# Input-row loads and mixer-row stores of 114 rows issued as 112 rows and 2 rows

## The chip, the core and the metric

The kernel runs on one core of one Trainium2 chip, as one program in one launch. The metric is the device time in microseconds; the time of before is the median of 3 runs. Five engines work side by side, each on its own instructions in order: PE (TensorE, matrix products into PSUM, with its weight loads PEld), DVE (VectorE), ACT (ScalarE), POOL (GpSimd) and SP (SyncE, which here only issues transfers between DRAM and the on-chip buffers). Engines wait for one another and for transfers by semaphores.

## What is computed

One layer of a hybrid decoder on 1024 rows of 1024 columns, with 16 learned rows ahead of them, all in float32. A mixer (a gated recurrence and a multi-window pooling, merged by sigmoid gates) gives `z`; its product with `w_out` is normalised and added to the input rows, and a gated FFN with a causal convolution of width 3 follows:

```python
h = jnp.concatenate([meta, x], axis=1)
...
z = (jax.nn.sigmoid(gate_a.astype(jnp.float32)) * (a @ w_branch_hgrn[l])
     + jax.nn.sigmoid(gate_b.astype(jnp.float32)) * (p @ w_branch_pool[l]))
h = h + rmsnorm(z @ w_out[l], mix_norm_post[l])
u = rmsnorm(h, ffn_norm_pre[l])
gt = causal_dwconv(u @ ffn_w_gate[l], ffn_conv_w[l], ffn_conv_b[l])
y = (jax.nn.gelu(gt, approximate=True) * (u @ ffn_w_up[l])) @ ffn_w_down[l]
h = h + rmsnorm(y, ffn_norm_post[l])
return h[:, N_META:]
```

## The kernel before

Every float32 product is made of three products of a split: an operand is cast to a high part (`hi`) by ACT, and DVE or POOL subtracts it from the operand for the low part (`lo`); `mm3` then issues hi-hi, hi-lo and lo-hi (L160 to L162, or L262 to L265 in the Strassen products).

The kernel goes through four stages: the projections and the recurrence (to about 600 us), the mixer's product with `w_out` (600 to about 730 us), the FFN's gate and up products in Strassen form (to about 1190 us), and the down product with the last norm.

The stage that matters is the second. Only 1026 of the 1040 rows are wanted from here on (`TQ`: the 1024 output rows and 2 rows of halo for the convolution). They are cut into three thirds of 342 rows (`c`), and each third into three row tiles of 342 / 3 = 114 rows (`RT`).

- `load_res` (L1000) loads the 114 input rows of a row tile, `row2` (written `row` in the profile), three tiles at the start of each third, called from `mix_mm`. The first tile of all takes 2 rows of `meta_tokens` and 112 of `x`.
- `mix_mm` (L1055) runs the third's product: for each of the 8 blocks `k` of `z` it takes a 128x1024 block of `w_out` (`wsplit`, L131: load `wraw`, cast `whi` on ACT, subtract `wlo` on POOL, on DVE for the last two), and 18 matmuls of 128x512 over the three row tiles into PSUM pairs `pm`. The blocks come from a `Loader` that is 3 ahead; `wraw`, `whi` and `wlo` have 3 buffers each. The blocks of `z` are split too (`split_z`, L935: `zc`), into the buffers of one large pool of 24 ("fm") that nearly everything shares, `m1`, `un` and `row2` too.
- `mix_out` (L1077) empties a third's PSUM pairs: ACT squares and sums a row tile (L1085, `junk`), DVE multiplies by the gain into `m1` (L1086, `m`). Two closures for each row tile follow, which are worked off between the blocks `k` of the next third: `vec` (L1090) forms the norm, adds the input rows (L1095), stores the 114 rows to the DRAM scratch `hs` (L1096, `hscr`) and normalises again to `un` (L340, L345); `feat` (L1099, by `to_quarters`) transposes `un` on PE (L1017, `pt`) and splits the result into the operands of the FFN (`v`, `t1` to `t4`, by `put`, L324 to L327, and L1032 to L1053).
- The last third's closures run between the first products of the FFN (`ffn.start_pair`), whose results DVE adds (`put_ffn`, L1191).
- The scratch `hs` is read back at the very end (`load_h`, L1351), 128 rows at a time.

All loads and stores named here are issued by SP, in one queue. The order of the rows on each engine is chosen by a scheduler that plays the program on a model of the chip; by hand it is fixed only in the first stage, and for POOL in the FFN. A change of any instruction can therefore move others.

Of the kernel before, what the change touches and what calls it, by code (L numbers as in the profile page):

```python
# [20 lines left out]
HALO = 2  # L21
# [35 lines left out]
def trunk_kernel(ctx: ExitStack, tc: tile.TileContext, x, meta_tokens, mix_norm_pre,  # L57
# [3 lines left out]
    nc = tc.nc  # L61
# [26 lines left out]
    def slot(n, dtype=F32, name="s"):  # L88
        return stage["fm", "p"].tile([P, n], dtype, tag="fm", name=nm(name), padded_shape=[P, L])
# [10 lines left out]
    def pair_banks(name="pt"):  # L100
        t = pair(name)
        return t[:, :512], t[:, 512:]
# [4 lines left out]
    def small(shape, name, tag, bufs=4):  # L107
        return sm.tile(shape, F32, tag=tag, name=nm(name), bufs=bufs)
# [55 lines left out]
    def proj(w, col, n_k, xs, chunks, ws=None, name="pj"):  # L164

        if ws is None:
            ws = wsplit(wblock(w, 0, n_k, col, P), n_k, P)
        whi, wlo = ws
        banks = [bank(name) for _ in chunks]
        for k in range(n_k):  # L170
            for (lo, n), ps in zip(chunks, banks):
                xhi, xlo = xs(k, lo, n)
                pe.matmul(ps[:, :n], whi[:, k, :], xhi, start=(k == 0), stop=False)
                pe.matmul(ps[:, :n], whi[:, k, :], xlo, start=False, stop=False)  # L174
            for (lo, n), ps in zip(chunks, banks):
                xhi, _ = xs(k, lo, n)
                pe.matmul(ps[:, :n], wlo[:, k, :], xhi, start=False, stop=(k == n_k - 1))
        return banks
# [151 lines left out]
    def row_rstd(ssq, rows, tag):  # L330
        std = small([P, 1], "std", tag + "s")
        act.activation(std[:rows], ssq[:rows], AF.Sqrt, bias=eps_t[:rows], scale=1.0 / D)
        rstd = small([P, 1], "rstd", tag + "r")
        dve.reciprocal(rstd[:rows], std[:rows])
        return rstd
# [12 lines left out]
    def norm_rows(row, rows, gbc):  # L348
        return list(norm_steps(row, rows, gbc))[-1]
# [498 lines left out]
    with tc.manual_schedule(engines={E.Activation, E.DVE, E.PE}):  # L848
# [59 lines left out]
        for h in range(EARLY_G):  # L908
            src, n_k, xs, chunks, post = job("G", h)
            r = proj(None, 0, n_k, xs, chunks, ws=gl.next(), name="pg")  # L910
# [65 lines left out]
    hs = dram.tile([TQ, D], F32, name="hscr")  # L976
# [11 lines left out]
    def add_quarters(*names):  # L988
        for q in names:
            for h in "hl":  # L990
# [4 lines left out]
    RT = CW // 3  # L995

    wo = Loader([(wblock(w_out[0], k, 1, 0, D), 1, D, dve if (c == 2 and k > 5) else pool_e)
                 for c in range(3) for k in range(KD)])

    def load_res(t0):  # L1000
        row = slot(D, name="row2")
        if t0 == 0:
            nc.sync.dma_start(row[:HALO], meta_tokens[T0:NM, :])
            nc.sync.dma_start(row[HALO:RT], x[0, 0 : RT - HALO, :])
        else:
            nc.sync.dma_start(row[:RT], x[0, t0 - HALO : t0 - HALO + RT, :])
        return row

    def t_tmp(n, name):
        return slot(n, name=nm(name))  # L1010

    def to_quarters(un, t_at, banks):

        for j in range(2):
            for i in range(4):
                k = 4 * j + i
                pe.transpose(banks[j][:, i * RT : (i + 1) * RT], un[:RT, k * P : (k + 1) * P], ident[:RT, :RT])  # L1017
        srcs = [b_[:, : 4 * RT].rearrange("p (k t) -> p k t", k=4) for b_ in banks]
        n1 = max(0, min(RT, HT - t_at))
        if n1:  # L1020
            for src, q in zip(srcs, ("b11", "b21")):
                put(q, src[:, :, :n1], slice(t_at, t_at + n1), dve)
        f = max(0, HT - HALO - t_at)
        n2 = RT - f
        if n2 <= 0:
            return
        d = slice(t_at + f - (HT - HALO), t_at + RT - (HT - HALO))
        b12, b22 = (src[:, :, f:] for src in srcs)

        t1, t2 = halves_tmp(n2)  # L1030
        c12, c22 = halves_tmp(n2)
        act.copy(c12, b12)  # L1032
        act.copy(c22, b22)
        combine(dve, t1, c12, ALU.subtract, "b11", d)
        dve.tensor_tensor(t2, c22, t1, ALU.subtract)
        put("t2", t2, d, dve)
        dve.tensor_tensor(c12, c22, c12, ALU.subtract)
        put("t1", t1, d, dve)
        put("b22", c22, d, pool_e)
        put("t3", c12, d, dve)  # L1040
        negdiff(t2, t2, "b21", d)
        return lambda: put("t4", t2, d, pool_e)
# [12 lines left out]
    def mix_mm(c, between, zs):  # L1055
        rows.update({c * CW + i * RT: load_res(c * CW + i * RT) for i in range(3)})
        banks = [pair_banks("pm") for _ in range(3)]
        znext = []
        for k in range(KD):
            whi, wlo = wo.next()  # L1060
            if k == KD - 1 and c < 2:
                znext = [split_z(c + 1, k_) for k_ in range(ZA)]
            zh, zl = zs[k]
            for i in range(3):
                t = slice(i * RT, (i + 1) * RT)
                for j in range(2):
                    n = slice(j * 512, (j + 1) * 512)
                    mm3(banks[i][j][:RT], (zh[:, t], zl[:, t]), (whi[:, 0, n], wlo[:, 0, n]), k == 0, k == KD - 1)
            wo.ahead()
            if k + ZA < KD:  # L1070
                zs.append(split_z(c, k + ZA))
            if between:
                for f in between.pop(0):
                    f()
        return banks, znext

    def mix_out(c, banks, g2, g3):  # L1077
        todo = []
        for i in range(3):
            m1 = slot(D, name="m1")  # L1080
            ssq = small([P, 2], "ssq2", "mq", 6)
            for j in range(2):
                n = slice(j * 512, (j + 1) * 512)
                junk = t_tmp(512, "junk")
                act.activation(junk[:RT], banks[i][j][:RT], AF.Square, accum_out=ssq[:RT, j : j + 1])  # L1085
                dve.tensor_tensor(m1[:RT, n], banks[i][j][:RT], g2[:RT, n], ALU.mult)  # L1086
            un = {}
            t0 = c * CW + i * RT

            def vec(i=i, m1=m1, ssq=ssq, un=un, t0=t0):  # L1090
                row = rows.pop(t0)
                s = small([P, 1], "mss", "ms")
                dve.tensor_tensor(s[:RT], ssq[:RT, 0:1], ssq[:RT, 1:2], ALU.add)
                rstd = row_rstd(s, RT, "m")
                dve.scalar_tensor_tensor(m1[:RT], m1[:RT], rstd[:RT], row[:RT], ALU.mult, ALU.add)  # L1095
                nc.sync.dma_start(hs[t0 : t0 + RT, :], m1[:RT])  # L1096
                un[0] = norm_rows(m1, RT, g3)

            def feat(un=un, t0=t0):  # L1099
                return to_quarters(un[0], t0, pair_banks())  # L1100

            todo += [vec, feat]
        return todo
# [325 lines left out]
```

## Time and profile before

| | |
|---|---|
| median of 3 runs | 1434.69 us (1431.66 to 1434.87) |
| profiled execution | 1431.93 us, its span 1430.1 us |
| mean granted PE clock | 0.979 |
| stores `hscr<-m` | 9 of 456 KB |
| loads `row<-in_x_dram` of `load_res` | 8 of 456 KB, 1 of 448 KB |
| 512 KB blocks of `w_out` | 24, landing after 3.1 to 20.3 us |

A profile line of the timeline gives the start (us from the span's start), the length in us, the engine, the line of the code, the operation, what is written and read (buffer numbers left out), and the count of merged instructions; in brackets the idle time of the engine before it and what ended that. SPq is SP's queue of issues: its lengths are those of the issue, not of the transfer.

### The profile page before, as it was taken

How to read it: one execution, taken by the hardware profiler on the slowest of the kernel's cores; microseconds unless marked ns; L12 is line 12 of the kernel's file. 1: busy time of each engine (PE TensorE's matmuls, PEld its weight loads, DVE VectorE, ACT ScalarE, POOL GpSimd, SP SyncE). 2: the span in 40 equal slices, each digit the busy share in tenths (PEclk: the TensorE clock that was granted, in tenths of full speed). 3: DMA queues.
4: the chain of work that ended last, by engine and by line, in shares of the span. 5: the costliest groups of instructions: out<-in, count | busy, mean ns of one | idle time of the engine just before them, and what ended most of it. 6: DMA issues, size and time to landing. Idle time of an engine off the chain costs nothing. (4 is left out here: it accounts for less than half of the span.)

```text
span 1430.1 us, 21631 instructions
## 1 busy us (share of the span) xinstructions
PE 1364.1 (95%) x8405; PEld 1233.2 (86%) x8405; DVE 976.1 (68%) x1406; ACT 570.1 (40%) x981; POOL 570.3 (40%) x400
## 2 busy tenths in 40 slices
PE   8989999999999999998968999999999999999976
PEld 6789999999999899976658888888899998888765
DVE  6784545489876754625678888888888775445476
ACT  6443333366654452244464322322222233333353
POOL 4255421237354410253348565544556642001051
PEclk9999999999999999999988999999999999999998
DMA  6034333321110033644542577666677798565546
GB/s 240 36 97 141 126 111 104 97 60 45 33 47 5 23 133 103 218 139 153 166 126 80 142 232 206 186 174 158 162 166 165 169 259 232 194 194 180 191 158 218
DMA packets 129562, 202.65 MB, mean 142 GB/s; under 512 B 7739, under 2 KB 75935, under 8 KB 129460
## 3 DMA queue, kind: packets, MB, share of 16 engines
q1 hardware_dynamic: 118548, 181.08, 37.9%
q0 software_dynamic: 10912, 20.19, 9.4%
q8 instruction: 66, 1.08, 0.3%
q14 instruction: 36, 0.29, 0.1%
HBM read 152.45 MB, written 71.85 MB: 157 GB/s over the span
## 5 line engine op out<-in xcount | busy, mean ns | idle before, releaser
L137 POOL TENSOR_TENSOR wlo<-wraw,whi 128x1024 fp32r<-128x1024 f32 (+2 forms) x37 | 85.3, 2311 | 228.2 <-ACT whi L136 146.5
L262 PE MATMUL P<-v,whi 128*128 128x258 f32 (+2 forms) x528 | 165.8, 328 | 10.9 <-DVE m L1086 4.3
L263 PE MATMUL P<-v,whi 128*128 128x258 f32 (+2 forms) x528 | 164.8, 325 | 0.7 <-POOL v L327 0.7
L265 PE MATMUL P<-v,wlo 128*128 128x258 f32 (+2 forms) x528 | 143.0, 325 | 0.0
L161 PE MATMUL pd<-rot 128*128 128x512 f32 x284 | 111.9, 394 | 8.6 <-DVE rot L1249 8.6
L262 PEld LDWEIGHTS P<-v,whi 128*128 128x128 f32 x528 | 103.1, 195 | 19.1 <-DVE m L1086 4.5
L136 ACT CAST whi<-wraw 128x1024 fp32r<-128x1024 f32 (+2 forms) x60 | 52.9, 884 | 158.6 <-PE pba L174 26.7
L162 PE MATMUL pd<-rot 128*128 128x512 f32 x284 | 111.3, 392 | 0.0
L263 PEld LDWEIGHTS P<-v,whi 128*128 128x128 f32 x528 | 103.1, 195 | 8.8 <-POOL v L327 1.0
L1249 DVE TENSOR_TENSOR rot<-yt,rot 128x1024 fp32r<-128x1024 f32 (+1 forms) x38 | 46.8, 1231 | 90.1 <-ACT rot L1248 90.1
L209 ACT CAST whi<-wraw 128x512 fp32r<-128x512 f32 x90 | 53.2, 617 | 109.6 <-PE P L263 94.4
L265 PEld LDWEIGHTS P<-v,wlo 128*128 128x128 f32 x528 | 90.0, 194 | 7.8
L1133 POOL TENSOR_TENSOR ys<-y 128x512 f32<-128x512 f32 x22 | 34.3, 1559 | 142.0 <-issue 99.4
L210 DVE TENSOR_TENSOR wlo<-wraw,whi 128x512 fp32r<-128x512 f32 x82 | 73.7, 921 | 18.2 <-ACT whi L209 18.2
L235 POOL TENSOR_TENSOR swa<-wraw,wraw 128x512 f32<-128x512 f32 x30 | 47.4, 1582 | 95.5 <-DMA wraw<-in_w_in_dram 62.3
L1248 ACT CAST rot<-yt 128x1024 fp32r<-128x1024 f32 (+1 forms) x38 | 37.7, 995 | 118.7 <-PE pd L161 118.7
L160 PE MATMUL pd<-rot 128*128 128x512 f32 x284 | 75.8, 390 | 1.2 <-ACT rot L1248 1.2
L161 PEld LDWEIGHTS pd<-rot 128*128 128x128 f32 x284 | 53.8, 190 | 21.5 <-DVE rot L1249 10.3
L209 ACT CAST whi<-swa 128x512 fp32r<-128x512 f32 x60 | 35.8, 618 | 87.8 <-PE P L263 74.9
L1183 DVE SCALAR_TENSOR_TENSOR y<-g,par,y 128x1024 f32<-128x1024 f32 x44 | 64.1, 1457 | 0.7
L160 PEld LDWEIGHTS pd<-rot 128*128 128x128 f32 x284 | 53.2, 188 | 12.7 <-ACT rot L1248 1.6
L162 PEld LDWEIGHTS pd<-rot 128*128 128x128 f32 x284 | 53.8, 190 | 11.2
(347 smaller groups left out, 4306.9 us busy)
## 6 DMA issues: line engine op xcount, KB each, us to landing
wraw<-in_w_in_dram SPq DMA_DIRECT2D x36, 512.0 KB, 3.5
yt<-ysum SPq DMA_DIRECT2D x33, 512.0 KB, 3.6
wraw<-in_ffn_w_gate_dram SPq DMA_DIRECT2D x26, 512.0 KB, 8.3
wraw<-in_w_out_dram SPq DMA_DIRECT2D x24, 512.0 KB, 8.7
wraw<-in_ffn_w_up_dram SPq DMA_DIRECT2D x22, 512.0 KB, 4.7
wsum<-in_ffn_w_down_dram SPq DMA_DIRECT2D x22, 512.0 KB, 5.9
ysum<-ys SPq DMA_DIRECT2D x11, 768.0 KB, 4.6
sa<-sscr SPq DMA_DIRECT2D x16, 513.0 KB, 5.2
```

Source lines behind the costliest of these rows:

```text
L136: act.copy(hi, raw)
L137: eng.tensor_tensor(lo, raw, rr(hi), ALU.subtract)
L160: pe.matmul(ps, ahi, bhi, start=first, stop=False)
L161: pe.matmul(ps, ahi, blo, start=False, stop=False)
L162: pe.matmul(ps, alo, bhi, start=False, stop=last)
L209: act.copy(hi, src)
L210: (pool_e if 4 <= i < 2 * self.early else dve).tensor_tensor(lo, src, rr(hi), ALU.subtract)
L235: pool_e.tensor_tensor(s1, a21, a22, ALU.add)
L262: pe.matmul(x[:, o : o + w], whi[:, k, :], xh[:, c : c + w], start=(k == 0), stop=False)
L263: pe.matmul(x[:, o : o + w], whi[:, k, :], xl[:, c : c + w], start=False, stop=False)
L265: pe.matmul(x[:, o : o + w], wlo[:, k, :], xh[:, c : c + w], start=False, stop=(k == 3))
L1183: dve.scalar_tensor_tensor(a, g[:, :, j : j + n], cvw[:, j, m : m + 1], a, ALU.mult, ALU.add)
```

## The change

Each transfer of 114 rows becomes two on the same queue, rows 0 to 111 and rows 112 to 113 of the tile. That holds for the 8 loads of `load_res` that were 114 rows (the ninth was already 2 and 112) and for the 9 stores of `vec`.

```diff
+    def by_rows(move):
+
+        for r in (slice(0, RT - HALO), slice(RT - HALO, RT)):
+            move(r)
+
     def load_res(t0):
...
-            nc.sync.dma_start(row[:RT], x[0, t0 - HALO : t0 - HALO + RT, :])
+            by_rows(lambda r: nc.sync.dma_start(row[r], x[0, t0 - HALO + r.start : t0 - HALO + r.stop, :]))
         return row
...
-                nc.sync.dma_start(hs[t0 : t0 + RT, :], m1[:RT])
+                by_rows(lambda r: nc.sync.dma_start(hs[t0 + r.start : t0 + r.stop, :], m1[r]))
```

Lines below L1006 move down by 5 in the changed kernel. The scheduler also moves rows of all engines between the second third of the mixer's product and the start of the FFN. Three places follow.

**First place: from the first to the second third, SP.** The rows are the input rows of the second third (`row_856` to `row_858`), the stores of the first third's last two tiles, and the next block of `w_out`. In brackets stand the semaphores that a row waits for; transfers take the eight of `DMAHW0` to `DMAHW7` in turn. Before:

```order
L1006 DMA row_856_6391<-in_x_dram 114x1024 [waits PE_49]
L1006 DMA row_857_6393<-in_x_dram 114x1024 [waits Activation_49]
L1006 DMA row_858_6395<-in_x_dram 114x1024 [waits Activation_49]
L1096 DMA hscr<-m_844_6375 114x1024 [waits DVE_49]
L1096 DMA hscr<-m_850_6383 114x1024 [waits DMAHW4_49,DVE_49]
L133 DMA wraw_6546<-in_w_out_dram 128x1024 [waits DMAHW5_49,Pool_49]
```

Now:

```order
L1011 DMA row_856_6393<-in_x_dram 112x1024 [waits PE_49]
L1011 DMA row_856_6393<-in_x_dram 2x1024
L1011 DMA row_857_6396<-in_x_dram 112x1024 [waits Activation_49]
L1011 DMA row_857_6396<-in_x_dram 2x1024 [waits DMAHW6_49]
L1011 DMA row_858_6399<-in_x_dram 112x1024 [waits DMAHW7_49,Activation_49]
L1011 DMA row_858_6399<-in_x_dram 2x1024 [waits DMAHW0_49]
L1101 DMA hscr<-m_844_6377 112x1024 [waits DMAHW1_49,DVE_49]
L1101 DMA hscr<-m_844_6377 2x1024 [waits DMAHW2_49]
L1101 DMA hscr<-m_850_6385 112x1024 [waits DMAHW3_49,DVE_49]
L1101 DMA hscr<-m_850_6385 2x1024 [waits DMAHW4_49]
L133 DMA wraw_6553<-in_w_out_dram 128x1024 [waits DMAHW5_49,Pool_49]
```

Five transfers became ten, and most of them carry a wait on a transfer's semaphore where two of six did.

**The same place on ACT:** the casts of the second third's `z` (`zc`), of the weight behind those transfers (`whi`), and of the first transposed row tile (`v<-pt`). Before:

```order
L938 CAST zc_6670<-sa_5610 128x342
L332 ACTIVATE std_6566<-ssq_6563,eps_t 114x1 [waits Activation_49]
L326 CAST v_787_6117<-pt_6515 128x4x114 [waits PE_49]
L938 CAST zc_6673<-sa_5661 128x342
L938 CAST zc_6676<-sa_5762 128x342 [waits DMAHW3_49,DVE_49]
L938 CAST zc_6679<-sa_5863 128x342 [waits DVE_49]
L326 CAST v_787_6117<-pt_6515 128x4x114 [waits DVE_49]
L136 CAST whi_6548<-wraw_6546 128x1024 [waits DMAHW5_49,PE_49,Pool_49]
L136 CAST whi_6592<-wraw_6590 128x1024 [waits DMAHW6_49,PE_49,Pool_49]
```

Now:

```order
L938 CAST zc_6678<-sa_5610 128x342 [waits DMAHW1_49,DMAHW0_49,DVE_49]
L332 ACTIVATE std_6574<-ssq_6571,eps_t 114x1 [waits Activation_49]
L938 CAST zc_6681<-sa_5661 128x342 [waits DMAHW2_49,DMAHW1_49,DVE_49]
L938 CAST zc_6684<-sa_5762 128x342 [waits DVE_49]
L136 CAST whi_6555<-wraw_6553 128x1024 [waits DMAHW5_49,PE_49,Pool_49]
L938 CAST zc_6687<-sa_5863 128x342
L326 CAST v_787_6117<-pt_6522 128x4x114 [waits PE_49]
L326 CAST v_787_6117<-pt_6522 128x4x114 [waits DVE_49]
L136 CAST whi_6600<-wraw_6598 128x1024 [waits DMAHW6_49,PE_49,Pool_49]
```

The waits of `zc` on transfers (`DMAHW3` before; `DMAHW0` to `DMAHW2` now) are for the stores of `m`, whose buffers they take. Both casts of `v` stand behind all four `zc` in the new order, and behind the cast of the weight `whi_6555` too.

**The same place on PE:** the transposes of the first row tile. Before:

```order
L160 MATMUL pm_6398<-whi_6420,zc_6340 114x512
L160 MATMUL pm_6399<-whi_6420,zc_6340 114x512
L1017 MATMUL pt_6515<-ident,un_6436 128x114 x8
L161 MATMUL pm_6397<-wlo_6421,zc_6340 114x512
L162 MATMUL pm_6397<-whi_6420,zc_6340 114x512
```

Now, the first four:

```order
L160 MATMUL pm_6403<-whi_6425,zc_6342 114x512
L160 MATMUL pm_6404<-whi_6425,zc_6342 114x512
L1022 MATMUL pt_6522<-ident,un_6442 128x114 x4
L161 MATMUL pm_6402<-wlo_6426,zc_6342 114x512
L162 MATMUL pm_6402<-whi_6425,zc_6342 114x512
```

and the second four:

```order
L162 MATMUL pm_6404<-whi_6425,zc_6342 114x512
L160 MATMUL pm_6402<-whi_6470,zc_6429 114x512
L1022 MATMUL pt_6522<-ident,un_6442 128x114 x4
L160 MATMUL pm_6403<-whi_6470,zc_6429 114x512
L160 MATMUL pm_6404<-whi_6470,zc_6429 114x512
```

Eight transposes stood together; now sixteen matmuls (rows of `pm_6402` to `pm_6404`) lie between the first four and the second four. In the third third (from `pt` of the second third's first row tile) the eight stay together.

**Second place: the last third's PSUM pairs, ACT.** The first square of the last third (`junk`) and what stands ahead of it, the casts for the FFN's operands. Before:

```order
L1032 COPY tt_1004_6992<-pt_6982 128x456 [waits PE_49]
L1033 COPY tt_1004_6992<-pt_6982 128x456
L326 CAST t4h_6919<-tt_994_6936 128x2x58 [waits Pool_49]
L326 CAST v_788_6118<-tt_1004_6992 128x4x114 [waits Activation_49]
L326 CAST t4h_6920<-tt_994_6936 128x2x58
L1085 ACTIVATE junk_1008_7099,ssq_1006_7098<-pm_6736 114x512 [waits DVE_49,PE_49]
```

Now:

```order
L1037 COPY tt_1004_7006<-pt_6996 128x456 [waits PE_49]
L1038 COPY tt_1004_7006<-pt_6996 128x456
L209 CAST whi_7145<-wraw_7135 128x512 [waits PE_49]
L209 CAST whi_7145<-wraw_7137 128x512
L326 CAST t4h_6933<-tt_994_6950 128x2x58 [waits Pool_49]
L326 CAST v_788_6118<-tt_1004_7006 128x4x114 [waits Activation_49]
L326 CAST v_788_6118<-tt_1002_7005 128x4x114 [waits DVE_49]
L326 CAST t4h_6934<-tt_994_6950 128x2x58
L326 CAST t3h_6929<-tt_1004_7006 128x2x114 [waits DVE_49]
L326 CAST t3h_6930<-tt_1004_7006 128x2x114
L1090 ACTIVATE junk_1008_7113,ssq_1006_7112<-pm_6747 114x512 [waits PE_49]
```

The square (L1085, now L1090) moved behind one more cast of `v` and both casts of `t3h`, and the casts of the FFN's first weights (`whi`) behind the copies of `pt`.

**Third place: the start of the FFN, DVE.** The adds of two pair products into a gate tile (L1191, now L1196) among the splits of the last row tile. Before:

```order
L1191 TENSOR_TENSOR g_7502<-p_1073_7373,P_1087_7473 128x514
L1047 TENSOR_TENSOR tt_1084_7451<-tt_1084_7451,v_787_6117 128x456
L1037 TENSOR_TENSOR tt_1086_7452<-tt_1086_7452 128x456
L1035 TENSOR_TENSOR tt_1084_7451<-tt_1086_7452,tt_1084_7451 128x456
L327 TENSOR_TENSOR v_788_6118<-tt_1084_7451,v_788_6118 128x4x114
L1191 TENSOR_TENSOR g_7531<-p_1073_7373,P_1091_7504 128x514
L210 TENSOR_TENSOR wlo_7583<-wraw_7376,whi_7582 128x512
L327 TENSOR_TENSOR t3l_6917<-tt_1086_7452,t3h_6915 128x2x114
L327 TENSOR_TENSOR t3l_6918<-tt_1086_7452,t3h_6916 128x2x114
L210 TENSOR_TENSOR wlo_7583<-wraw_7547,whi_7582 128x512
L327 TENSOR_TENSOR t2l_6913<-tt_1084_7451,t2h_6911 128x2x114
L327 TENSOR_TENSOR t2l_6914<-tt_1084_7451,t2h_6912 128x2x114
```

Now:

```order
L1052 TENSOR_TENSOR tt_1084_7468<-tt_1086_7469,v_787_6117 128x456
L210 TENSOR_TENSOR wlo_7516<-swb_7396,whi_7515 128x512
L1052 TENSOR_TENSOR tt_1084_7468<-tt_1084_7468,v_787_6117 128x456
L1042 TENSOR_TENSOR tt_1086_7469<-tt_1086_7469 128x456
L1196 TENSOR_TENSOR g_7519<-p_1073_7390,P_1087_7490 128x514
L1040 TENSOR_TENSOR tt_1084_7468<-tt_1086_7469,tt_1084_7468 128x456
L327 TENSOR_TENSOR v_788_6118<-tt_1084_7468,v_788_6118 128x4x114
L327 TENSOR_TENSOR t3l_6931<-tt_1086_7469,t3h_6929 128x2x114
L327 TENSOR_TENSOR t3l_6932<-tt_1086_7469,t3h_6930 128x2x114
L327 TENSOR_TENSOR t2l_6927<-tt_1084_7468,t2h_6925 128x2x114
L327 TENSOR_TENSOR t2l_6928<-tt_1084_7468,t2h_6926 128x2x114
L1196 TENSOR_TENSOR g_7548<-p_1073_7390,P_1091_7521 128x514
```

The first of the two adds moved behind two steps on `tt`, and the second (`g_7531`, now `g_7548`) from ahead of the splits `t3l` and `t2l` to behind them.

## Prediction

> **What bounds the kernel now.** Every number here is of one profiled execution. I read the page first, for the share of each engine, then the table of stretches.
>
> ```profile
> span 1430.1 us, 21631 instructions
> PE 1364.1 (95%) x8405; PEld 1233.2 (86%) x8405; DVE 976.1 (68%) x1406; ACT 570.1 (40%) x981; POOL 570.3 (40%) x400
> ...
> 605.00:735.00 130.00, 115.94 (x509) 88.03 (x507) 74.54 (x108) 62.08 (x130) 58.20 (x28) 0.95 0.47 151
> 860.00:1190.00 330.00, 330.00 (x2067) 297.57 (x2067) 271.34 (x324) 95.16 (x152) 177.15 (x132) 1.00 0.71 183
> ```
>
> The columns of a stretch are its length, then busy time (and instructions) of PE, PEld, DVE, ACT and POOL, the granted PE clock, the DMA share and GB/s. PE sets the time. From 860 to 1190 us it never stops, so what it gains earlier reaches the end in full. The transfers of the change run between 600 and 750, and there PE is idle or below full clock part of the time. PE's timeline says where; the bracket gives the idle time before a row and what ended it.
>
> ```profile
> 655.12 0.61 PE L1017 MATMUL pt<-ident,un 114*128 114x114 f32 x4 [2.14 <-DVE un L345]
> 670.15 1.75 PE L1017 MATMUL pt<-ident,un 114*128 114x114 f32 x8 [2.90 <-DVE v L327]
> 675.72 0.49 PE L161 MATMUL pm<-wlo,zc 128*114 128x512 f32 x1 [0.93 <-POOL wlo L137]
> 699.03 0.61 PE L1017 MATMUL pt<-ident,un 114*128 114x114 f32 x4 [0.97 <-DVE un L345]
> 701.79 1.02 PE L1017 MATMUL pt<-ident,un 114*128 114x114 f32 x4 [2.15 <-DVE un L345]
> 718.09 0.49 PE L160 MATMUL pm<-whi,zc 128*114 128x512 f32 x1 [0.39 <-ACT whi L136]
> 719.35 0.49 PE L161 MATMUL pm<-wlo,zc 128*114 128x512 f32 x1 [0.77 <-DVE wlo L137]
> 735.68 0.58 PE L262 MATMUL P<-v,whi 128*128 128x258 f32 x1 [4.33 <-DVE m L1086]
> 746.75 0.99 PE L1017 MATMUL pt<-ident,un 114*128 114x114 f32 x4 [5.56 <-DVE un L345]
> ```
>
> An idle spell of some 2 us is followed by slow matmuls:
>
> ```profile
> 656.54 0.63 PE L162 MATMUL pm<-whi,zc 128*114 128x512 f32 x1
> 659.92 0.39 PE L160 MATMUL pm<-whi,zc 128*114 128x512 f32 x1
> ...
> 671.58 0.75 PE L161 MATMUL pm<-wlo,zc 128*114 128x512 f32 x1
> 673.70 0.39 PE L160 MATMUL pm<-whi,zc 128*114 128x512 f32 x1
> 674.39 0.40 PE L160 MATMUL pm<-whi,zc 128*114 128x512 f32 x1
> 680.90 0.94 PE L1017 MATMUL pt<-ident,un 114*128 114x114 f32 x8
> ```
>
> Eight matmuls fill 656.54 to 659.92 (0.42 us each) and five 671.58 to 673.70 (0.42); the three from 673.70 to 674.39 take 0.23 each. So a slow matmul costs 0.19 us more, and eight transposes 1.75 instead of 0.94.
>
> **Who is late behind these waits.** The wait at 670.15 names DVE, but DVE (the subtract behind the cast of `v`) waited for ACT, and ACT for a transfer:
>
> ```profile
> 668.02 0.86 ACT L938 CAST zc<-sa 128x342 fp32r<-128x342 f32 x2 [9.46 <-DMA hscr<-m]
> 716.99 1.05 ACT L136 CAST whi<-wraw 128x1024 fp32r<-128x1024 f32 x1 [8.32 <-DMA wraw<-in_w_out_dram]
> ...
> 643.80 0.29 SPq L1096 DMA_DIRECT2D hscr<-m  x1
> 644.56 3.65 SPq L1006 DMA_DIRECT2D row<-in_x_dram  x3
> 648.26 3.25 SPq L1096 DMA_DIRECT2D hscr<-m  x2
> 651.79 32.08 SPq L133 DMA_DIRECT2D wraw<-in_w_out_dram  x7
> ...
> 664.00:672.00 8.00, 5.09 (x24) 4.03 (x23) 1.48 (x3) 1.29 (x3) 0.00 (x0) 0.88 0.38 157
> 708.00:716.00 8.00, 8.00 (x41) 6.24 (x40) 0.73 (x2) 0.54 (x1) 0.00 (x0) 1.00 0.39 157
> wraw<-in_w_out_dram SPq DMA_DIRECT2D x4, 512.0 KB, 20.3
> wraw<-in_w_out_dram SPq DMA_DIRECT2D x11, 512.0 KB, 3.3
> GB/s 295 426 393 98 229 229 229 197 66 131 98 262 393 426 393 328 426 426 393 426 393 393 459 393 459 393 393 426 426 426 262 295 197 328 197 164 164 98 131 98
> ```
>
> At 668.02 ACT writes a `zc` into a buffer that a store of `m` still had to leave; that store was issued at 648.26 or soon after. Both last stretches show a DMA share of 0.38 or 0.39 at 157 GB/s, for 8 us: six engines of sixteen are 0.375. The last line, 600 to 605 us, peaks at 390 to 460 GB/s with all at work. The two lines above it count issues and median landing: four `w_out` blocks issued in 644 to 660 landed after 20.3 us, eleven in 590 to 640 after 3.3. So each transfer of 114 rows occupies six engines, and a weight block split over sixteen queues behind its share on those six. The sum agrees: three loads and three stores of 456 KB (466,944 bytes) are 2.80 MB, at 157 GB/s 17.8 us, and 6/16 of four weight blocks add 5.0: from 644 to 667.
>
> The Trainium skill (DMA: Bandwidth & Descriptors, "Why a DMA increments its semaphore by 16 and not by 1") says that a transfer runs on the largest number of engines up to 16 that divides its slowest dimension: six for 114, 16 for 112, two for 2. By that rule the change does what it says, and the share of 0.38 agrees for the 114.
>
> **The change, part by part.**
>
> *Transfers.* Eight loads and nine stores become 17 of 112 rows and 17 of 2. If the 112 rows spread like the 128-row ones, 2.80 MB and four weight blocks (2.10 MB) need 12 us at 400 GB/s, so everything issued from 643.8 has landed by about 656, before ACT gets to the `zc` at 658.6 (668.02 less 9.46). Weight blocks then land in about 3.3 us.
>
> The nearest rows bound what that is worth. (a) At 670.15: 2.90 idle, 0.81 of slow transposes, five slow matmuls (0.95): 4.7 us. (b) At 675.72: the weight block issued at 651.79 is the one that landed after 20.3 us; 0.93 goes. (c) At 718: 0.39 + 0.77 = 1.2. Below, each could be nothing if ACT gets stuck elsewhere. I take all three, 6.8 us: the next thing late is the pair of weights through ACT (1.05 us a cast) and POOL, which at 3.3 us landing kept up with PE in the first third of the mixer's product, where no PE wait is listed.
>
> (d) The last third's evacuation. ACT, 8.32 us late at 716.99, starts the squares of the last three row tiles late:
>
> ```profile
> 728.32 0.28 PE L262 MATMUL P<-v,whi 128*128 128x258 f32 x1
> 730.54 0.59 ACT L1085 ACTIVATE junk<-pm 114x512 f32<-114x512 f32 x1
> 636.32 0.60 ACT L1085 ACTIVATE junk<-pm 114x512 f32<-114x512 f32 x1 [0.29 <-PE pm L162]
> ```
>
> PE's product begins at 728.32, and twelve matmuls at 0.23 lie between the end of the first row tile and it, so the square could have begun at 725.5; it began 5.0 later. In the first third (636.32) it began 0.29 after PE. With ACT on time the waits at 735.68 and 746.75 shrink by up to 5.0. But the new order puts two `t3h` casts ahead of this square (they wait for DVE), so I take 2.0.
>
> *Order.* The scheduler moved rows too. (e) The second four transposes of the first row tile now stand sixteen matmuls (3.7 us) later on PE. Their operand was 2.14 late at 655.12, so the wait should be covered, with the eight slow matmuls behind it (1.5): 3.6 us, or nothing if `un` is later too. What makes `un` late stays:
>
> ```profile
> 648.96 5.56 POOL L137 TENSOR_TENSOR wlo<-wraw,whi 128x1024 fp32r<-128x1024 f32 x2 [6.26 <-ACT whi L136]
> 649.41 5.66 DVE L345 SCALAR_TENSOR_TENSOR un<-m,rstd,g 114x512 f32<-114x512 f32 x2
> 660.57 1.40 DVE L345 SCALAR_TENSOR_TENSOR un<-m,rstd,g 114x512 f32<-114x512 f32 x2
> ```
>
> Two `un` halves take 5.66 us beside POOL's subtracts, 1.40 alone. No transfer is in that, so the waits at 699.03 and 701.79, whose transposes stay together, remain: 3.1 idle, and slow matmuls behind them for another 1.5 as in (e). I leave both in.
>
> (f) At the start of the FFN, DVE's add of the fourth pair product is now behind the splits of `t3` and `t2`:
>
> ```profile
> 771.78 0.98 DVE L210 TENSOR_TENSOR wlo<-swb,whi 128x512 fp32r<-128x512 f32 x1 [2.92 <-ACT whi L209]
> 778.98 2.20 DVE L327 TENSOR_TENSOR t3l<-tt,t3h 128x228 fp32r<-128x228 f32 x2
> 782.10 2.88 DVE L327 TENSOR_TENSOR t2l<-tt,t2h 128x228 fp32r<-128x228 f32 x2
> ```
>
> It can free its PSUM pair up to 5.1 us later; or nothing, since those splits are wanted as well and DVE stood idle 2.92 just ahead. I charge 2.0.
>
> *New issues and waits.* SP gets 17 more issues, 0.3 us each by the store at 643.80, 5 us in all, in a queue that otherwise waits; nothing of it is on PE's path unless a weight block is late. Each DMA takes one of eight semaphores in turn and waits until the transfer eight before it has landed; SP's weight block behind the ten pieces waits so too. On ACT the casts of `v` now stand behind the cast of that weight (`whi_6555`): with 3.3 us of landing it is there by about 656, and PE wants the `v` only for the next transposes, 51 matmuls (11.9 us) after 653.
>
> *Sum.* 6.8 + 2.0 + 3.6 - 2.0 = 10.4 us. The profiled execution took 1431.9 us, 1.8 more than its span; it becomes 1421.5. The median of the runs shown, 1434.69, lies 2.8 higher, so the forecast is 1424.
>
> **Rivals.**
>
> *More goes* (1415): with less of a backlog on ACT and DVE, the waits at 699.03 and 701.79 go too (3.1 + 1.5), (d) gives all of its 5.0, and (f) costs nothing: 10.4 + 4.6 + 3.0 + 2.0 = 20.0 us less. The end of this side is all nine PE waits listed above, 20.1 us, with some 5 of slow clock: 1410. For it: in 664 to 672 and 708 to 716 DVE is busy 2.2 us of 16, so it has room to be ahead. Against: POOL's subtracts make `un` late, and they stay.
>
> *Given back* (1433): (f) costs its full 5.1, and (e) and (d) bring nothing: 6.8 - 5.1 = 1.7 us less. For it: both (d) and (f) depend on DVE, and the new order puts more ahead of what PE wants. Against: the work is the same and begins earlier.
>
> *The spread is not the cause* (1431): the transfers are slow for another reason, and only (e) is gained, 3.6. The Trainium skill (DMA: Bandwidth & Descriptors, "Rules for kernel authors") says that two transfers to disjoint partitions aren't worth it, as both use the same sixteen engines, and that under 64 KB one pays mostly overhead; the 8 KB pieces are that. By this rule nothing is gained from the split; the share of 0.38 speaks against its first half here.
>
> *Slower* (1448): the ring of eight semaphores. From 644.56 ten pieces go out in a row, and most of them wait for the transfer eight before. If a piece lands only after 20.3 us, as the four weight blocks did, ten take 25 us, and the next weight block is issued at about 670. PE wants that weight at about 665 (the 51 matmuls after 653), and 3.3 of landing, 1.05 of cast and 2.8 of subtract (half of POOL's 5.56) lie ahead of it: the rival decides from an issue at 658, that is from pieces that land in 10.7 us. At 670 PE waits 12 us, in two of the three thirds. These 24 stand in place of (a) to (c) and take 3.6 of (e) off: 24 - 6.8 - 3.6 = 13.6 slower. For it: the waits stand in the order. Against: where no such jam was, the eleven blocks landed in 3.3.
>
> **How the numbers follow.** Forecast 0.57 (1424, own range 1417 to 1430), more goes 0.13, given back 0.16, spread not the cause 0.06, slower 0.08. A measurement of this kernel tells 0.3% (4.3 us) from no change. Faster than 1430.4: the first two and a quarter of the third, 0.74. Same: the rest of the third and the fourth, 0.18. Slower: 0.08. The range takes in both ends of the first four cases and leaves out the last: 1410 to 1434.
>
> **What would show it.** In the profile after: no stretch at a share of 0.38; `w_out` blocks landing in 3 to 5 us throughout; no `zc` cast waiting for `hscr` and no `whi` waiting over 1 us for `w_out`; no PE waits at the places of 670, 675 and 718; none before the second four transposes; the waits at 699 and 701.79 still there. Wrong would be: `w_out` still landing after 10 us or more, SP standing at the pieces, or the start of the FFN losing what the stage before it gained.

## The result, and the profile after

| | before | after |
|---|---|---|
| median | 1434.78 us (1431.66 to 1434.91, 4 runs) | 1417.39 us (1416.58 to 1417.51, 4 runs) |
| after / before | | 0.9883, 95% interval 0.9866 to 0.9900 |
| profiled execution, its span | 1431.93, 1430.1 us | 1416.58, 1414.8 us |
| mean granted PE clock | 0.979 | 0.985 |

The change makes the kernel 17.4 us faster. The forecast was a gain of 10.7 (to 1424), so the sign held and the size was short: 1417.39 lies on the lower edge of the forecast's own range (1417 to 1430) and nearer to the rival "more goes" (1415). One execution of a kernel below, `rows102`, took 4698 us, and its median and ratio are those of the other nine.

The head of the page of after:

```profile
span 1414.8 us, 21656 instructions
PE 1356.0 (96%) x8405; PEld 1226.9 (87%) x8405; DVE 983.2 (69%) x1406; ACT 570.4 (40%) x981; POOL 566.3 (40%) x400
```

PE does the same 8405 matmuls with 8.1 us less busy time (1364.1 before: fewer of them at a low clock) and idles less. Where, PE's timeline of after says: these are its waits, and one group of transposes that begins without any.

```profile
654.21 0.61 PE L1022 MATMUL pt<-ident,un 114*128 114x114 f32 x4 [0.15 <-DVE un L345]
668.91 0.97 PE L1022 MATMUL pt<-ident,un 114*128 114x114 f32 x8 [1.89 <-DVE v L327]
692.03 0.94 PE L1022 MATMUL pt<-ident,un 114*128 114x114 f32 x8
702.68 0.97 PE L1022 MATMUL pt<-ident,un 114*128 114x114 f32 x8 [1.27 <-DVE v L327]
721.93 0.39 PE L262 MATMUL P<-v,whi 128*128 128x258 f32 x1 [2.83 <-DVE m L1091]
732.17 0.99 PE L1022 MATMUL pt<-ident,un 114*128 114x114 f32 x4 [5.60 <-DVE un L345]
749.21 0.39 PE L262 MATMUL P<-v,whi 128*128 128x258 f32 x1 [0.98 <-DVE g L1196]
762.01 0.58 PE L262 MATMUL P<-v,whi 128*128 128x256 f32 x1 [6.34 <-ACT v L326]
763.34 0.58 PE L262 MATMUL P<-v,whi 128*128 128x258 f32 x1 [0.76 <-DVE g L1196]
```

The waits for weights (675.72 and 718 before) are gone, and so are those for `un` in the first two handoffs (655.12, 699.03 and 701.79 before). The wait for `v` at the first handoff is 1.89 instead of 2.90, and its transposes take 0.97 instead of 1.75. At the start of the FFN the long wait stands at another place (762.01).

On the transfer side, ACT's rows of after that waited for a block of `w_out`, SP's next issue of weights at the first handoff, and one stretch (its last two columns are the DMA share and GB/s):

```profile
653.90 1.05 ACT L136 CAST whi<-wraw 128x1024 fp32r<-128x1024 f32 x1 [0.25 <-DMA wraw<-in_w_out_dram]
693.12 1.05 ACT L136 CAST whi<-wraw 128x1024 fp32r<-128x1024 f32 x1 [0.34 <-DMA wraw<-in_w_out_dram]
...
656.80 21.21 SPq L133 DMA_DIRECT2D wraw<-in_w_out_dram  x7
...
652.00:660.00 8.00, 7.85 (x39) 5.84 (x39) 8.00 (x5) 4.43 (x9) 7.22 (x3) 1.00 0.99 301
```

ACT waits 0.6 us in all where it waited 8.32 at once, and no `zc` cast waits for a store. The handoff's transfers run at a share of 0.99. The next weight block is issued at 656.80, 5.0 later than before (1.8 of it since the whole stage starts later) and 1.2 ahead of the 658 that the rival "slower" needed. SP's waits of after in 600 to 740 (us in total, times, longest) show what else held it:

```profile
SPq L1101 <- DMA wraw<-in_w_out_dram: 3.4, 1, 3.4
SPq L1101 <- DMA row<-in_x_dram: 1.8, 2, 1.5
```

The 3.4 and the 1.5 lie between 650 and 656: the second and the third piece of the stores wait for the transfers that are eight ahead of them in the queue, the first of these a weight block issued at 646.39. So the ring of eight does hold SP here, and a weight block took some 7 us to land, not the 3 to 5 that the prediction asked for throughout.

### The profile page after: what moved, and what is told of

Same layout as the page of the kernel before. It is cut to its first block, busy times and chain, and to the rows that moved or that the text cites. A ratio compares the mean times of both kernels' runs of the same rounds, so it can differ in the third digit from the quotient of the medians.

```text
span 1414.8 us, 21656 instructions
## 1 busy us (share of the span) xinstructions
PE 1356.0 (96%) x8405; PEld 1226.9 (87%) x8405; DVE 983.2 (69%) x1406; ACT 570.4 (40%) x981; POOL 566.3 (40%) x400
```

## The experiments

Three questions: is it the spread over the engines or the new order of rows; how much of the spread is needed; and what are the extra issues worth. "Jam" is short for the stretch in which transfers of 114 rows stand on six engines. Where a kernel is said to have the order of another, every engine runs the same operations in the same order. Ratios are to the kernel before, on the same chip in the same session; its median in the three sessions was 1433.87, 1432.90 and 1432.28.

| kernel | loads, stores (rows) | order | median us | ratio, 95% interval |
|---|---|---|---|---|
| `rows112` | 112, 112 | before | 1417.21 | 0.9886 (0.9866 to 0.9906) |
| `rows102` | 102, 102 | before | 1430.64 | 0.9978 (0.9968 to 0.9989) |
| `p102` | 102+12, 102+12 | after | 1431.23 | 0.9988 (0.9978 to 0.9998) |
| `half57` | 57+57, 57+57 | after | 1464.02 | 1.0213 (1.0194 to 1.0233) |
| `stores` | 114, 112+2 | a third | 1419.42 | 0.9912 (0.9894 to 0.9929) |
| `load128` | 128, 112+2 | that third | 1419.98 | 0.9914 (0.9899 to 0.9929) |
| `loads` | 112+2, 114 | nearly after | 1416.28 | 0.9880 (0.9863 to 0.9897) |
| `pieces16` | 7 x 16 + 2, both | a fourth | 1431.10 | 0.9988 (0.9979 to 0.9998) |
| `l128` | 128, 114 | before | 1421.52 | 0.9932 (0.9919 to 0.9945) |
| `l128s112` | 128, 112 | before | 1422.30 | 0.9935 (0.9922 to 0.9947) |
| `loads_again` | as `loads` | nearly after | 1415.80 | 0.9888 (0.9873 to 0.9902) |
| `after_again` | as after | after | 1416.63 | 0.9889 (0.9876 to 0.9901) |

### Spread or order

**`rows112`**, the spread in the order of before (it leaves out the last two rows of each tile):

```diff
+    nc.sync.dma_start(hs.rearrange("(n r) d -> n r d", r=RT)[:, RT - HALO :, :], x[0, : 9 * HALO, :].rearrange("(n r) d -> n r d", r=HALO))
...
-            nc.sync.dma_start(row[:RT], x[0, t0 - HALO : t0 - HALO + RT, :])
+            nc.sync.dma_start(row[:112], x[0, t0 - HALO : t0 - HALO + 112, :])
...
-                dve.scalar_tensor_tensor(m1[:RT], m1[:RT], rstd[:RT], row[:RT], ALU.mult, ALU.add)
-                nc.sync.dma_start(hs[t0 : t0 + RT, :], m1[:RT])
+                dve.scalar_tensor_tensor(m1[:112], m1[:112], rstd[:112], row[:112], ALU.mult, ALU.add)
+                nc.sync.dma_start(hs[t0 : t0 + 112, :], m1[:112])
```

> This kernel has the rows of before, in the order of before on every engine; its loads and stores of 114 rows are single transfers of 112, and the last two rows of each tile are not loaded, added or stored (one early transfer of 72 KB fills their place in the scratch tensor). So it has the spread without the new order and without the 17 small pieces. Spread theory (transfers of 114 rows on six of sixteen engines hold the weight blocks and a zc buffer back, and that is most of the gain): no stretch at a DMA share of 0.38 in 644 to 667, weight blocks landing in 3 to 6 us, no PE wait at the places of 670, 675 and 718; 17.4 us less the 3.6 of the moved transposes, so about 1421, at most 1427. Order theory (the new order of rows is most of the gain, the spread little): within 4 us of before, 1431 to 1437.

**`rows102`**, its control: the same edit with 102 for 112 (it leaves out twelve).

> The control of the kernel with 112 rows: the order of before, single transfers of 102 rows (102 = 6 x 17, so six engines by the spread theory), the last twelve rows of each tile not loaded, added or stored (one early transfer of 432 KB fills their place in the scratch tensor). Both theories: as before, 1430 to 1436 (a tenth less to move at the same rate is 2 us of a jam of 23), with the stretch at a share of 0.38 and w_out landing in 15 to 20 us in 644 to 660. If it is as fast as the kernel with 112 rows, the time went with the rows left out and not with the spread, and the spread theory falls.

**`p102`**, the order of after with the jam:

```diff
-        for r in (slice(0, RT - HALO), slice(RT - HALO, RT)):
+        for r in (slice(0, 102), slice(102, RT)):
```

> The kernel after with the rows split 102 and 12 instead of 112 and 2: the same order on every engine as after, the same number of pieces. 102 rows go on six engines by the divisor rule, 12 rows on twelve. Spread theory: the share of 0.38 is back, w_out lands in 15 us or more, and the time is that of before or more, 1428 to 1440 (3.6 may remain of the order, but the casts of v now stand behind a weight that lands late). Order theory: the time of after, 1415 to 1420.

**`half57`**, the order of after with half as many engines:

```diff
-        for r in (slice(0, RT - HALO), slice(RT - HALO, RT)):
+        for r in (slice(0, RT // 2), slice(RT // 2, RT)):
```

> The kernel after with the rows split 57 and 57: the same order on every engine as after, the same number of pieces of 228 KB. 57 = 3 x 19, so three engines a piece. Spread theory: if the two pieces take the same three engines the jam is twice that of before, a share near 0.19 at some 79 GB/s, w_out landing in some 40 us, and two handoffs lose some 20 us each: 1455 to 1475; if the two pieces run on different engines it is as before, 1430 to 1440. Order theory: the time of after, 1415 to 1420.

Measured: 1417.21, 1430.64, 1431.23 and 1464.02. Sixteen engines in the old order give what after has, six engines in the new order give almost nothing, and three engines make it 30 us slower. The order theory, that the order is most of the gain, falls; what the order adds to the spread comes out in the fourth part. `rows112` came out 4 us below what the spread theory expected of it, which the fourth part takes up.

The jam of `half57`: a stretch, SP's queue, and PE's waits at the two handoffs:

```profile
652.00:660.00 8.00, 7.95 (x39) 6.24 (x40) 7.58 (x8) 2.66 (x5) 4.88 (x2) 1.00 0.19 79
...
644.60 10.83 SPq L1011 DMA_DIRECT2D row<-in_x_dram  x6
655.53 11.79 SPq L1101 DMA_DIRECT2D hscr<-m  x4
667.42 28.64 SPq L133 DMA_DIRECT2D wraw<-in_w_out_dram  x6
...
690.79 1.76 PE L1022 MATMUL pt<-ident,un 114*128 114x114 f32 x8 [25.92 <-DVE v L327]
741.30 1.62 PE L160 MATMUL pm<-whi,zc 128*114 128x512 f32 x3 [16.09 <-ACT whi L136]
```

A share of 0.19 is three engines of sixteen (0.1875), although all six pieces of the loads were issued by 655.5: pieces of 57 rows queue on the same three. Here SP stands too: the issues of six pieces of the loads take 10.83 us and those of four pieces of the stores 11.79 (2.31 and 6.92 in after), and the next weight goes out at 667.42. So the rival "slower" has its effect here, a weight block issued late behind slow pieces, though by longer issues: no wait of SP for a landing is listed in that stretch.

In `p102`, ACT's waits for transfers at the first handoff, and PE's waits:

```profile
666.54 0.86 ACT L938 CAST zc<-sa 128x342 fp32r<-128x342 f32 x2 [8.76 <-DMA hscr<-m]
670.47 1.04 ACT L136 CAST whi<-wraw 128x1024 fp32r<-128x1024 f32 x1 [3.07 <-DMA wraw<-in_w_out_dram]
...
654.06 0.61 PE L1022 MATMUL pt<-ident,un 114*128 114x114 f32 x4 [0.16 <-DVE un L345]
676.23 1.75 PE L1022 MATMUL pt<-ident,un 114*128 114x114 f32 x8 [9.36 <-DVE v L327]
```

The new order took the wait for `un` of 2.14 at 655 down to 0.16, as in after, and the wait for `v` grew from 2.90 to 9.36. In `rows102` no wait for `un` is listed there either, and that for `v` has grown to 5.41:

```profile
669.63 1.75 PE L1018 MATMUL pt<-ident,un 114*128 114x114 f32 x8 [5.41 <-DVE v L327]
```

While the jam lasts, PE ends up waiting for the same landing, and what is saved ahead of it is paid there. In `p102` 652 to 660 has a share of 0.44 at 159 GB/s, where after has 0.99 at 301; the ring holds SP there too, and the next weight goes out at 660.57 only.

### How much of the spread is needed

**`stores`** and **`loads`** split only the one or the other:

```diff
# stores
-            by_rows(lambda r: nc.sync.dma_start(row[r], x[0, t0 - HALO + r.start : t0 - HALO + r.stop, :]))
+            nc.sync.dma_start(row[:RT], x[0, t0 - HALO : t0 - HALO + RT, :])
# loads
-                by_rows(lambda r: nc.sync.dma_start(hs[t0 + r.start : t0 + r.stop, :], m1[r]))
+                nc.sync.dma_start(hs[t0 : t0 + RT, :], m1[:RT])
```

> Only the stores are split into 112 and 2; the loads stay single transfers of 114 rows on six engines. The row order is that of the next kernel on every engine. By the jam of before, the three loads of a handoff are 1.40 MB, 8.9 us at 157 GB/s, half of what stood on the six engines. Proportional theory (each transfer of 114 rows costs its share of the 17 us): about 1426. Threshold theory (the jam costs only what outlasts the slack of the zc cast at about 658.6 and of the weight that PE wants at about 665): issued from 644.6 to 648.3, the loads are gone by about 656, little is left, 1417 to 1421.

> Only the loads are split into 112 and 2; the stores stay single transfers of 114 rows on six engines. Proportional theory: about 1426. Threshold theory: the stores are the later half of the jam (the second and third are issued at 648.3 or soon after, the weight block right behind them), 0.93 MB at 157 GB/s is 5.9 us, gone by about 656 with the weight block a few us behind: 1417 to 1422, a little more than with only the stores split, since the zc buffer waits for just these stores.

**`load128`** has the order of `stores` and the loads on sixteen engines as well:

```diff
-            by_rows(lambda r: nc.sync.dma_start(row[r], x[0, t0 - HALO + r.start : t0 - HALO + r.stop, :]))
+            n = min(P, SEQ + HALO - t0)
+            nc.sync.dma_start(row[:n], x[0, t0 - HALO : t0 - HALO + n, :])
```

> As the kernel with only the stores split, in the same order on every engine with the same number of issues, but each load is one transfer of 128 rows (14 more than needed, so the load is on sixteen engines; the last tile of all loads what is left, 114). The difference between these two is the spread of the loads alone. Proportional theory: 8 us faster than the one with only the stores split. Threshold theory: within 4 us of it. Both: the time of after, 1415 to 1420, with eight pieces of 8 KB fewer.

**`l128`** is the kernel before with that load alone:

```diff
-            nc.sync.dma_start(row[:RT], x[0, t0 - HALO : t0 - HALO + RT, :])
+            n = min(P, SEQ + HALO - t0)
+            nc.sync.dma_start(row[:n], x[0, t0 - HALO : t0 - HALO + n, :])
```

> The kernel before with one thing changed: a load is one transfer of 128 rows instead of 114 (the last tile 114), so it is on sixteen engines. The order is that of before on every engine, no issue is added, and the stores stay single transfers of 114 rows on six. Threshold theory (half of the jam gone is nearly all of the gain, as with only the loads split, 1416.3): 1415 to 1422, weights landing in 3 to 7 us. Proportional theory: 1424 to 1427.

Measured: 1419.42 and 1416.28 with either half split; 1419.98 with the loads spread as well, no faster than `stores`; and 1421.52 for `l128` against 1422.30 for `l128s112`, which spreads the stores too. Half of the jam gone is all of the gain that the spread gives, three times over; the proportional theory (1424 to 1427) falls. `loads` came out below the 1417 to 1422 of the threshold theory, and ahead of `stores` where it was expected behind; the two differ in the waits for `un`, which the fourth part takes up. `l128` shows the slack. Its stores are still on six engines, and landing isn't back to the 3 to 7 us expected; the row counts the blocks issued in 644 to 660 and their median landing, and ACT's rows follow:

```profile
wraw<-in_w_out_dram SPq DMA_DIRECT2D x3, 512.0 KB, 11.5
...
660.46 0.48 ACT L938 CAST zc<-sa 128x342 fp32r<-128x342 f32 x1 [0.68 <-DMA hscr<-m]
664.59 1.05 ACT L136 CAST whi<-wraw 128x1024 fp32r<-128x1024 f32 x1 [2.14 <-DMA wraw<-in_w_out_dram]
```

The `zc` cast waits 0.68 instead of 9.46 and the weight's cast 2.14, and no PE wait for `v` or a weight follows. With blocks landing after 11.5 us and the `zc` buffer free 0.68 late, PE waits for neither; with 20.3 and 9.46 it did.

### What the extra issues cost

**`pieces16`**, 102 issues more than after:

```diff
-        for r in (slice(0, RT - HALO), slice(RT - HALO, RT)):
+        for r in [slice(i, min(i + 16, RT)) for i in range(0, RT, 16)]:
```

> Each transfer of 114 rows in eight pieces of 16 rows and fewer (seven of 64 KB and one of 8 KB), 102 issues more than after; the row order moves in places too. It asks what an issue costs once the spread is there (16 rows go on sixteen engines). Some 48 pieces stand on SP at a handoff ahead of the next weight block. Issue-bound theory (0.3 to 0.4 us each and no wait for the ring of eight): 14 to 19 us from 645, the weight goes out near 662 instead of 656.8, 4 us past the point of 658 from which PE waits: 1420 to 1428. Ring theory (each piece also waits for the landing of the one eight before, as the stores of after, 6.92 us for four, suggest: 1.7 us each): the weight goes out 30 to 80 us late, 1460 or more. Free theory: 1415 to 1420.

Measured: 1431.10, 14.5 more than after. SP's queue, the pieces' median landing (of those issued in 644 to 660), and PE's waits at the first handoff:

```profile
646.80 11.10 SPq L1011 DMA_DIRECT2D row<-in_x_dram  x24
663.59 1.10 SPq L133 DMA_DIRECT2D wraw<-in_w_out_dram  x2
...
row<-in_x_dram SPq DMA_DIRECT2D x21, 64.0 KB, 2.2
...
666.13 1.75 PE L1022 MATMUL pt<-ident,un 114*128 114x114 f32 x8 [3.77 <-DVE v L327]
668.54 1.62 PE L160 MATMUL pm<-whi,zc 128*114 128x512 f32 x3 [0.66 <-ACT whi L136]
```

Pieces that land in 2.2 us don't hold SP at a ring of eight; an issue takes 0.46 us (11.10 / 24), above the 0.3 to 0.4 expected, and the weight goes out at 663.59, past the 658 worked out in the prediction. So it is the issue-bound theory with a dearer issue, and its 1420 to 1428 was missed. The ring theory falls for these pieces. The 14.5 us are not the price of the issues alone, since the order differs too: at the second handoff PE waits 6.9 us, 2.3 of them for a copy on ACT (`tt`), where after waits 1.3.

**`loads_again`** and **`after_again`**, those two kernels unchanged, side by side:

> Only the loads split, once more, beside the kernel after on the same chip, to see whether the eight or nine issues that it has fewer are worth anything. If an issue of 0.3 us on SP costs PE nothing: within 0.2% of after. If the stores' pieces hold a weight up: 2 to 4 us faster than after.

> The kernel after, unchanged, beside the other three on the same chip: 1416 to 1419 by every theory. The other ratios are read against this one.

Measured: 1415.80 and 1416.63, ratios 0.9888 and 0.9889. The nine issues fewer are worth nothing that can be told, so no version tried beats after; `loads` does as well with half of the edit.

### The rest: who is caught beside POOL

**`l128s112`** was to show why `rows112` was faster than expected:

```diff
# l128, with the first line of rows112, and
-                nc.sync.dma_start(hs[t0 : t0 + RT, :], m1[:RT])
+                nc.sync.dma_start(hs[t0 : t0 + RT - HALO, :], m1[: RT - HALO])
```

> As the last, and the stores are single transfers of 112 rows (the last two rows of each tile are computed and not stored; one early transfer of 72 KB fills their place), so nothing is left on six engines, in the order of before. It differs from the kernel with 112 rows everywhere in that DVE adds all 114 rows. Theory that the un halves are caught beside POOL's subtracts by the number of rows that DVE works on ahead of them: the waits of about 0.9 and 2.1 us for un are back at both handoffs and the time is 1419 to 1422. Theory that it hangs on the transfers: no such waits, 1415 to 1419.

Measured: 1422.30, 5.1 more than `rows112`, which has the same order and no jam either. PE's waits in 600 to 760, by what they were for (us in total, times, longest), of `l128s112` and of after; before's, from its rows in the prediction, are 10.8 for `un` (2.14, 0.97, 2.15, 5.56), 4.3 for `m`, 2.9 for `v` and 2.1 for weights:

```profile
PE pt L1019 <- DVE un L345: 10.8, 4, 5.6
PE P L262 <- DVE m L1088: 2.8, 1, 2.8
```

```profile
PE pt L1022 <- DVE un L345: 5.8, 2, 5.6
PE pt L1022 <- DVE v L327: 3.2, 2, 1.9
PE P L262 <- DVE m L1091: 2.8, 1, 2.8
PE P L262 <- DVE g L1196: 1.0, 1, 1.0
```

Taking the jam away removes every wait for a transfer and leaves all 10.8 of `un`; the new order then removes 5.0 of those and brings 3.2 for `v`. The other kernels sort the same way. `stores` and `load128`, in the third order, have the waits of before for `un` (2.14 to 2.15 at the first handoff, 0.91 and 2.14 at the second) and take 1419 to 1420; `loads` and `loads_again`, nearly in the order of after, have none at either handoff and take 1416. How the `un` halves escape shows at the second handoff, in DVE's and POOL's timelines of `l128s112`, after and `rows112`:

```profile
691.01 5.65 DVE L345 SCALAR_TENSOR_TENSOR un<-m,rstd,g 114x512 f32<-114x512 f32 x2
690.71 8.19 POOL L137 TENSOR_TENSOR wlo<-wraw,whi 128x1024 fp32r<-128x1024 f32 x3 [7.29 <-ACT whi L136]
```

```profile
689.15 7.02 DVE L345 SCALAR_TENSOR_TENSOR un<-m,rstd,g 114x512 f32<-114x512 f32 x4
689.93 8.51 POOL L137 TENSOR_TENSOR wlo<-wraw,whi 128x1024 fp32r<-128x1024 f32 x3 [6.74 <-ACT whi L136]
```

```profile
688.00 1.41 DVE L345 SCALAR_TENSOR_TENSOR un<-m,rstd,g 114x512 f32<-114x512 f32 x2
687.70 9.56 POOL L137 TENSOR_TENSOR wlo<-wraw,whi 128x1024 fp32r<-128x1024 f32 x3 [7.29 <-ACT whi L136]
```

In after, `un` starts 0.78 ahead of POOL's subtracts, and PE's eight transposes at 692.03 find the first tile ready. In `l128s112` POOL starts 0.30 ahead, two halves take 5.65, and PE waits twice. In `rows112` POOL also starts 0.30 ahead, and yet two halves take 1.41, and POOL's three subtracts 9.56 instead of 8.19: here POOL was the one to wait. In all three kernels with the order of before and adds of 114 rows (before, `l128`, `l128s112`) the first halves are caught, in both with shorter adds (`rows112`, `rows102`) they aren't. The expectation on the adds' rows held for the waits (2.14 at the first handoff, 0.98 and 2.15 at the second; the time came out just above its 1419 to 1422), but loads and adds were shortened together there, and what decides this race isn't shown.

The Trainium skill (SBUF — State Buffer, "SBUF: two separate sides") says that a DVE operation with two inputs in SBUF and a POOL operation that reads SBUF share one pair of ports as an exclusive lock: whichever starts first has it for the whole instruction, and the other is blocked. The rows agree on the block, since the 1.4 that POOL's subtracts take longer in `rows112` are what the two halves take. They don't show who comes first by the starts of the records, which are the same in both; DVE's add ahead of `un`, with two inputs as well, was still running when POOL's record began in both (until 691.09 and 688.07).

## Why the prediction was right, and where its size was off

Two stretches of PE's timeline separate the terms: from the first `w_out` product to the first FFN product, and from there to the end of the span. Their starts, of before, of `l128s112` and of after (before's second is in the prediction):

```profile
605.56 0.39 PE L160 MATMUL pm<-whi,zc 128*114 128x512 f32 x1
...
606.27 0.39 PE L160 MATMUL pm<-whi,zc 128*114 128x512 f32 x1
720.39 0.28 PE L262 MATMUL P<-v,whi 128*128 128x258 f32 x1
...
607.40 0.39 PE L160 MATMUL pm<-whi,zc 128*114 128x512 f32 x1
716.07 0.28 PE L262 MATMUL P<-v,whi 128*128 128x258 f32 x1
```

With spans of 1430.1, 1419.5 and 1414.8 the stretches are 122.8, 114.1 and 108.7 for the first, 701.8, 699.1 and 698.7 for the second. (After started the stage 1.8 later than before, which is the difference between the sum below and the spans.)

| term | forecast, us | measured, us |
|---|---|---|
| (a) to (c), transfers late in the mixer | 6.8 | 8.6, before to `l128s112`, first stretch |
| (d), last third's evacuation | 2.0 | 2.7, same, second stretch |
| (e) with the `un` waits of the second handoff | 3.6 | 5.4, `l128s112` to after, first stretch |
| (f), DVE's order at the start of the FFN | -2.0 | 0.4, same, second stretch |
| sum | 10.4 | 17.1 |

**The mechanism held.** The share of 0.38 was six engines, weights and a store were late behind it, and PE waited for those: `l128`, which changes nothing but the rows of a load, takes the 2.90 for `v` and the three waits for weights away. The Trainium skill's rule that the prediction drew on (DMA: Bandwidth & Descriptors, "Why a DMA increments its semaphore by 16 and not by 1"), the largest divisor up to 16, agrees with the traces: 0.38 for 114 rows and 0.19 for 57. The other rule (the Trainium skill, DMA: Bandwidth & Descriptors, "Rules for kernel authors": two transfers to disjoint partition halves aren't worth it, under 64 KB mostly overhead) doesn't decide here: its reason, that both use all sixteen engines, doesn't hold for 114 rows, and the 8 KB pieces cost nothing that can be told, as `loads_again` with nine of them fewer takes 1415.80 beside 1416.63. The pieces of `pieces16` are of 64 KB and don't test its second half.

**(a) to (d) were sized a little low**, 8.8 against 11.3 by the profiles and 10.0 by the medians of one session (1432.28 and 1422.30). In (d) the wait for `m` shrank by 1.5, from 4.33 to 2.8; the rest lies behind it, but not at the wait for `un` of 5.56, which the prediction had shrink too and which is 5.57 in `l128s112`.

**The step that failed is the one on order**: "No transfer is in that, so the waits at 699.03 and 701.79, whose transposes stay together, remain". No transfer is in it, as `l128s112` shows, where the waits for `un` still sum to 10.8 without any jam. But it doesn't follow that they remain: the scheduler's new order starts `un` ahead of POOL's subtracts there. With these in, the third line is 5.4 and not 3.6. The order also gave something back that the prediction put at nothing: the casts of `v` moved back on ACT, and PE waits 1.89 and 1.27 for `v` at the two handoffs, where `l128s112` doesn't wait. The weight ahead of these casts isn't there by about 656; it's issued at 656.80. The first cast of `v` starts at 663.71, and DVE puts two subtracts of `zc` ahead of its own for `v`:

```profile
663.85 3.13 DVE L939 TENSOR_TENSOR zc<-sa,zc 128x342 fp32r<-128x342 f32 x2
666.91 0.62 DVE L327 TENSOR_TENSOR v<-pt,v 128x456 fp32r<-128x456 f32 x1
```

So two more signs that the prediction named did not come: the place of 670 kept a wait, and the places of 699 and 701.79 lost theirs. And (f) was charged 2.0 that PE didn't pay: the three waits at the FFN's start are 0.98 + 6.34 + 0.76 = 8.1 in after, and the four of before sum to 8.1 too (4.13 + 0.68 + 0.86 + 2.44):

```profile
773.50 0.55 PE L262 MATMUL P<-v,whi 128*128 128x258 f32 x1 [4.13 <-DVE g L1191]
775.17 0.58 PE L263 MATMUL P<-v,whi 128*128 128x256 f32 x1 [0.68 <-POOL v L327]
783.62 0.39 PE L263 MATMUL P<-t2l,whi 128*128 128x256 f32 x1 [0.86 <-DVE t2l L327]
791.71 0.49 PE L262 MATMUL P<-v,whi 128*128 128x512 f32 x1 [2.44 <-DVE g L1193]
```

Of the 6.7 us by which the sum was short, 4.2 are in (e) and (f).

**The sum of single waits was safe only because all went together.** `p102` shows that (e) is worth next to nothing while (a) stands, and `rows102`, whose `un` comes in time too, shows the same, since PE waits for the same landing later. Forecasting (e) alone, as the rival "the spread is not the cause" did with 3.6, was too much: `p102` is that kernel, with the issues of after, and it gains 0.0012 of the time, some 1.7 us (0.3 to 3.2).

**The rivals.** "More goes" was right on the waits at 699 and 701.79 and on (f), and wrong on its reason: not a smaller backlog but the order took them, and (d) gave 2.7 of its 5.0. "Given back" did not come. "Slower" had its mechanism: the ring does hold SP in after (3.4 and 1.5), and a weight goes out late in `half57`, where SP stands at slow pieces, and in `pieces16`, where it stands at many. But with 112 and 2 rows it goes out at 656.80, ahead of the point from which the rival decides, by 1.2 us or, counted from the start of the stage, 3.0.

## What to carry to other kernels

In these kernels a transfer's row count decided how many DMA engines it held: look for a plateau of the DMA share at a simple fraction (0.38 for 114 rows, 0.19 for 57) and for other transfers that land late beside it. The jam cost only what outlasted the slack, so taking away half of it gave all that the spread gives, and rounding a load up to 128 rows, with no issue added, gave 10.8 of the 15.7 us of that session. Before adding up waits on one engine, ask which of them end with the same late landing. And when the order changes, ask again when operations that collide will start, not only whether both are still there.

## What the runs showed of the hardware

- Pieces of 57 rows stay at a share of 0.19 with several of them issued, as those of 114 stay at 0.38 in before: here transfers of one row count queue on the same engines and leave the others idle.
- With the jam half gone (`l128`), weight blocks landed after 11.5 us (median of three) and PE didn't wait; at 20.3 (before) it did.
- Issues of 64 KB pieces took 0.46 us each on SP (24 in 11.10, `pieces16`), where the single store of before took 0.29.
- The same two `un` halves take 1.41 us (`rows112`) or 5.65 (`l128s112`) beside POOL's subtracts, with the same order and the same 0.30 us of POOL's lead. What decides it stays open.
